# One place moved to each half of the split weights: four instead of three for high and low parts, eight instead of ten for raw chunks of the experts' weights

## The chip, the cores and the metric

The kernel runs on one core of a Trainium2 chip. The metric is the device time of one execution in microseconds (us). The engines are named as in the profile: PE (TensorE, matrix products), PEld (its loading of stationary operands), DVE (VectorE), ACT (ScalarE), POOL (GpSimd) and SP (SyncE, which here only issues loads). L1316 is line 1316 of the kernel.

## The reference, cut to what matters

The kernel computes one layer of a decoder trunk for 512 tokens of width 1024: a token mixer of three branches, cross-attention, and a mixture of experts. Only the last is touched. Each token goes to 4 of 32 experts; an expert is a gated unit with a 1024x2048 and a 1024x1024 weight matrix in float32.

```
def moe_ffn(h, w_router, b_router, w_gu, b_gu, w_down, b_down):
    ...
    top_logits, top_idx = lax.top_k(logits, TOP_K)
    gates = jax.nn.softmax(top_logits.astype(jnp.float32), axis=-1).astype(t.dtype)
    ...
    def expert_block(args):
        xb, e = args
        gu = xb @ w_gu[e] + b_gu[e]
        return clamped_swiglu(gu[:, :D_FF], gu[:, D_FF:]) @ w_down[e] + b_down[e]
    ...
    y = jnp.zeros_like(t).at[tok_of].add(y_assign)
```

## The kernel before

**Chunks.** The experts' weights (384 MB) come as 384 chunks of 128x2048 float32, 1 MB each (8 KB per partition): eight for w_gu and four for w_down of an expert. `chunk_raw` (L1312) takes the next raw place and issues the load on SP's queue (L1316). The raw places are taken in turn from three pools: mraw0 with 2, mraw1 with 5 and mraw2 with 3, ten in all. A load that takes a place waits on SP, in order, until the last reader of that place ten chunks earlier is done.

**High and low parts.** For most chunks `chunk` (L1319) makes two operands that PE can multiply at its faster rate: ACT writes the high part mhi (L114), DVE subtracts it from the raw chunk and writes the low part mlo (L115). Both have three places (pool mhl). PE multiplies the high part with the high and low part of the tokens, the low part with the high part alone. A place is free again when PE has read it.

```
def hl_tile(self, j):
    pool, k, n = self.hl_turns[self.nhl[j] % len(self.hl_turns)]
    self.nhl[j] += 1
    t = ("mhi", "mlo")[j] + str(k)
    return pool.tile([128, 2048], F32R, name=t, tag=t, bufs=n)
```

**Two streams.** Experts are walked in two interleaved streams (`run`, L1543). Stream A has 17 experts, 14 of them with 96 rows of tokens; their w_gu gate half is partly multiplied straight from the raw chunk in plain float32 (`mraw,xF` in the rows). Stream B has 15 experts with 64 rows; there the high and low part of the tokens stand side by side as 128 rows (xgN). From about 1443 us on the work repeats every two experts: 24 chunks, one wide expert and one narrow one. A repetition is called a period below.

**What an expert needs besides chunks.** `prepare` (L1409) finds the expert's tokens: DVE compares slot numbers (Pe, L1232 or L1237), PE multiplies (pt<-V,Pe), DVE writes the table of rows GI and the gates GT (L1244, L1245), and POOL issues an indirect load that gathers the tokens' rows, 4 KB each (L1592, xg<-x_scratch,GI). PE transposes what was gathered (L110, pt<-ident,xg: xg_10070, called xg1 in the program, for stream A, and xg0 for stream B), and ACT and DVE split it (xgT and xF, or xgN). After `gate` (L1444) and `up` (L1462) the product g is transposed (pt<-ident,g) and split into hT, in two halves. After `down` (L1494) the output o of an expert is added to memory by an indirect store with addition, also issued by POOL (L1597, y_scratch<-o,GI).

**What sets the order.** These steps are not written into the loop where they run: `when` (L1383) notes a step with the number of splits and of chunks after which it is due, and `flush` (L1388) runs what is due, placed behind the newest split. The program is then put in order for each engine by a scheduler that uses times of its own, and each engine runs its instructions in that order. POOL's indirect loads and stores thus stand in one row too.

Of the kernel before, what the change touches and what calls it, by code (L numbers as in the profile page):

```python
# [92 lines left out]
class K:  # L93
# [1236 lines left out]
    def moe(self, wk, xgp):  # L1330
# [212 lines left out]
        def run(T):  # L1543
# [3 lines left out]
            for e, f, g in zip(T, [*T[1:], None], [*T[2:], None, None]):  # L1547
# [10 lines left out]
                if f not in (None, 31):  # L1558
                    yield from up(f)

        A, B = [run(T) for T in STREAMS]
        a = b = True
        for n in range(999):
# [233 lines left out]
    def run(self):  # L1797
        nc, I, ctx = self.nc, self.I, self.ctx
        self.raws = []
        self.hls = []  # L1800

        self.newest = {}
        self.ths = {}
        dram = lambda n, shape, dt=F32: nc.dram_tensor(n, shape, dt, kind="Internal").ap()
        self.x0d = dram("x0_scratch", (NT, 128, D))
        self.kTd = dram("kx_scratch", (128, KT, 256))
        self.x2d = dram("x2_scratch", (S, D))
        self.y2d = dram("y2_scratch", (S, D))
        self.tabd = dram("blk_scratch", (NX, 2))
        self.tabid = dram("blki_scratch", (NX, 1), I32)  # L1810
        self.setup()
        wpc = ExitStack()
        self.wp = wpc.enter_context(self.pool("w", bufs=3, side="right"))
        with ExitStack() as pc:
            self.pd = pc.enter_context(self.pool("pd", bufs=2, space=PSUM))
            self.ps = pc.enter_context(self.pool("ps", bufs=2, space=PSUM))
            self.pt = pc.enter_context(self.pool("pt", bufs=2, space=PSUM))
            self.po = pc.enter_context(self.pool("po", bufs=2, space=PSUM))
            mgc, xc = ExitStack(), ExitStack()
            self.mixers(mgc)  # L1820
            xT = xc.enter_context(self.pool("xT"))
            x1p = xc.enter_context(self.pool("x1"))
            R, xh = self.mix_out(x1p, xT)
            mgc.close()
            rc = ExitStack()

            def before_xo():
                wpc.close()
                self.mp = ctx.enter_context(self.pool("moe", side="right"))
                self.moe_setup(self.mp)  # L1830
                self.hl_pool(ctx.enter_context(self.pool("mhl", side="right")), 3)
                self.raw_pool(ctx.enter_context(self.pool("mraw0", side="right")), 2)

            def x2_done(i):
                if i == 0:
                    self.route_setup(rc.enter_context(self.pool("route")))
                nc.scalar.dma_start(self.x2d[i * 128:i * 128 + 128], R[i])
                nc.gpsimd.dma_start(self.y2d[i * 128:i * 128 + 128], R[i])
                self.route_tile(i, R[i])
                if "x2" in self.dbg:  # L1840
                    nc.sync.dma_start(self.dbg["x2"][i], R[i])
            self.xattn(R, xh, xT, ExitStack(), x2_done, before_xo)
            self.route()
            rc.close()
            self.gp2.close()
            xc.close()
        with ExitStack() as pc:
            self.pd = pc.enter_context(self.pool("pd", bufs=3, space=PSUM))
            self.pt = pc.enter_context(self.pool("pt", bufs=2, space=PSUM))
            xgp = pc.enter_context(self.pool("mxg"))  # L1850
            self.raw_pool(pc.enter_context(self.pool("mraw2")), 3)
            wk = pc.enter_context(self.pool("mwk"))
            self.moe(wk, xgp)
        self.more_blocks()
# [74 lines left out]
```

## Time and profile before

| | |
|---|---|
| time, median of 3 runs | 2422.8 us (2421.11 to 2424.07) |
| the profiled execution | 2424.83 us, of which span 2423.0 us |
| mean granted clock of PE | 0.965 of full speed |
| busy share of the span: PE, DVE, ACT, POOL | 93%, 72%, 53%, 17% |
| the experts' stage | about 1240 to 2423 us |
| loads | 531 MB in all, 384 MB of them the chunks |

The busy shares are means over stages that differ. PE's matrix products are pipelined and their ends modelled, so a busy PE says little; what an engine waits for, and between which two instructions, says more.

### The profile page before, as it was taken

To read this page: it belongs to the slowest core of one execution; us is meant where nothing else is said; L and a number is where in the kernel's file an instruction comes from. 1 tells how busy PE (TensorE), PEld (TensorE's weight loads), DVE (VectorE), ACT (ScalarE), POOL (GpSimd) and SP (SyncE) were. 2 spreads that over 40 slices of the span, in tenths; PEclk is the share of its full clock that TensorE was granted. 3 is DMA by queue.
4 is the path that set the end of the run, shared out by engine and by line. 5 is a ranking of instruction groups with operands and counts; after the bars stand their busy time and mean duration, and the time that the engine had idled before them with its cause. 6 is when DMAs were issued, how large, how long until landed. Compare 5 with 4: busy or idle time off the path is not lost.

```text
span 2423.0 us, 29556 instructions
## 1 busy us (share of the span) xinstructions
PE 2245.9 (93%) x10449; PEld 1666.4 (69%) x10449; DVE 1745.0 (72%) x2696; ACT 1295.6 (53%) x1744; POOL 403.9 (17%) x289
## 2 busy tenths in 40 slices
PE   7999899999999998999899999999999999999893
PEld 6778789878887776787776666565666666555552
DVE  6465577546668675535757998888888888889886
ACT  3444433345557563123235777666667666667662
POOL 2000133121010002001301251202212211221102
PEclk9999899999999999999779999999999999999996
DMA  8432222332221214243639999999999999999992
GB/s 262 113 83 70 66 65 67 97 97 70 70 68 37 62 35 126 74 131 120 246 120 359 386 390 383 371 371 368 370 368 361 363 377 366 366 365 342 374 326 77
DMA packets 258792, 530.84 MB, mean 219 GB/s; under 512 B 31047, under 2 KB 143940, under 8 KB 258512
## 3 DMA queue, kind: packets, MB, share of 16 engines
q1 hardware_dynamic: 244720, 487.89, 57.3%
q0 software_dynamic: 11904, 33.61, 5.6%
q10 hardware_dynamic: 2016, 7.41, 0.9%
q8 instruction: 84, 1.38, 0.2%
q14 instruction: 68, 0.56, 0.1%
HBM read 507.70 MB, written 19.40 MB: 218 GB/s over the span
## 4 chain that ended last, share of the span: by engine, by line
PE 62%; DVE 15%; issue 12%; DMA 5%; ACT 4%; POOL 1%; DVEq 0%; SPq 0%; ACTq 0%; POOLq 0%
PE pd L107 49%; DVE mlo L115 7%; PE ps L107 5%; PE pt L110 4%; PE po L107 4%; ACT mhi L114 3%; DMA y_scratch<-o,GI 2%; PE pt L107 1%; DVE wlo L115 1%; DVE g L1476 1%; DMA mraw<-in_w_xo_dram 1%; DVE g L1453 1%; DMA raw<-in_w_xq_dram 1%; DMA xg<-x_scratch,GI 0%; DVE g L1459 0%
## 5 line engine op out<-in xcount | busy, mean ns | idle before, releaser
L115 DVE TENSOR_TENSOR mlo<-mraw,mhi 128x2048 fp32r<-128x2048 f32 x320 | 726.7, 2280 | 72.1 <-ACT mhi L114 67.2
L114 ACT ACTIVATE mhi<-mraw 128x2048 fp32r<-128x2048 f32 x323 | 606.6, 1908 | 66.9 <-PE pd L107 42.0
L107 PE MATMUL pd<-hT,whi 128*128 128x512 f32 (+1 forms) x1136 | 296.8, 406 | 9.0 <-DVE qs L352 4.2
L1597 POOL DMA_INDIRECT y_scratch<-o,GI x31 | 157.7, 5087 | 755.7 <-DVE o L1508 378.4
L107 PEld LDWEIGHTS pd<-hT,whi 128*128 128x128 f32 (+1 forms) x1136 | 213.2, 192 | 58.5 <-issue 3.9
L115 DVE TENSOR_TENSOR wlo<-raw,whi 128x1024 fp32r<-128x1024 f32 (+1 forms) x121 | 155.5, 1288 | 126.9 <-ACT whi L114 59.8
L107 PE MATMUL pd<-mraw,xF 128*96 128x512 f32 (+1 forms) x512 | 231.1, 593 | 0.0
L114 ACT ACTIVATE whi<-raw 128x1024 fp32r<-128x1024 f32 (+1 forms) x121 | 127.2, 1058 | 187.4 <-PE pd L107 144.4
L107 PE MATMUL pd<-mhi,hT 128*96 128x512 f32 (+1 forms) x720 | 193.0, 402 | 21.0 <-DVE hT L115 14.3
L107 PEld LDWEIGHTS pd<-mhi,hT 128*96 128x96 f32 (+1 forms) x720 | 121.4, 173 | 70.4 <-DVE hT L115 16.8
L107 PE MATMUL pd<-mlo,hT 128*128 128x512 f32 (+1 forms) x496 | 149.5, 423 | 18.0 <-DVE mlo L115 18.0
L107 PEld LDWEIGHTS pd<-mraw,xF 128*96 128x96 f32 (+1 forms) x512 | 79.5, 158 | 113.3 <-issue 107.4
L107 PE MATMUL pd<-hT,wlo 128*128 128x512 f32 (+1 forms) x568 | 156.6, 401 | 0.0
L107 PE MATMUL pd<-mlo,xgN 128*128 128x512 f32 x480 | 137.2, 407 | 12.3 <-DVE mlo L115 11.4
L107 PE MATMUL pd<-mhi,xgT 128*96 128x512 f32 (+1 forms) x544 | 141.2, 400 | 3.3 <-ACT mhi L114 1.6
L107 PE MATMUL pd<-mhi,xgN 128*128 128x512 f32 x480 | 134.6, 402 | 0.1
L107 PEld LDWEIGHTS pd<-mlo,hT 128*128 128x128 f32 (+1 forms) x496 | 83.6, 179 | 72.4 <-DVE mlo L115 40.8
L107 PEld LDWEIGHTS pd<-hT,wlo 128*128 128x128 f32 (+1 forms) x568 | 104.9, 188 | 22.8 <-issue 0.7
L107 PEld LDWEIGHTS pd<-mhi,xgT 128*96 128x96 f32 (+1 forms) x544 | 90.5, 168 | 40.5 <-ACT mhi L114 2.4
L107 PEld LDWEIGHTS pd<-mlo,xgN 128*128 128x128 f32 x480 | 86.0, 188 | 46.8 <-DVE mlo L115 26.3
L115 DVE TENSOR_TENSOR ptl<-pt,pth 128x512 fp32r<-128x512 f32 (+4 forms) x144 | 84.6, 606 | 44.0 <-ACT pth L114 42.9
L114 ACT ACTIVATE pth<-pt 128x512 fp32r<-128x512 f32 (+4 forms) x144 | 72.3, 527 | 69.2 <-PE pt L110 68.3
(445 smaller groups left out, 3812.7 us busy)
## 6 DMA issues: line engine op xcount, KB each, us to landing
mraw<-in_w_gu_dram SPq DMA_DIRECT2D x256, 1024.0 KB, 9.1
mraw<-in_w_down_dram SPq DMA_DIRECT2D x128, 1024.0 KB, 7.7
raw<-in_w_in_dram SPq DMA_DIRECT2D x78, 512.0 KB, 4.1
kd<-kd POOLq DMA_DIRECT2D x20, 256.0 KB, 4.2
raw<-in_w_xk_dram SPq DMA_DIRECT2D x8, 512.0 KB, 9.1
raw<-in_w_in_dram SPq DMA_DIRECT2D x16, 256.0 KB, 3.5
raw<-in_w_br_b_dram SPq DMA_DIRECT2D x8, 512.0 KB, 3.9
raw<-in_w_br_c_dram SPq DMA_DIRECT2D x8, 512.0 KB, 3.9
```

The costliest lines, as they stand in the source:

```text
L107: return self.nc.tensor.matmul(out, l, r, start=start, stop=stop)
L110: self.nc.tensor.transpose(out, in_, self.ident[:n, :n])
L114: return (self.nc.scalar.activation(hi, src, AF.Copy), (eng or self.nc.vector).tensor_tensor(lo, src, hi.bitcast(F32), op=ALU.subtract))
L115: (eng or self.nc.vector).tensor_tensor(lo, src, hi.bitcast(F32), op=ALU.subtract))
L1453: nc.vector.tensor_scalar(g, P, 7.0, None, op0=ALU.min)
L1476: nc.vector.tensor_tensor(g[:, c], u, g[:, c], op=ALU.mult)
L1597: self.nc.gpsimd.indirect_dma_start(out=self.y2d, out_offset=bass.IndirectOffsetOnAxis(ap=GI, axis=0), in_=o, in_offset=None, bounds_check ...
```

## The change

In the scope that runs the experts' stage, the third raw pool shrinks from three places to one, and a pool with one place for a high part and one for a low part is opened beside it. A raw place, a high place and a low place are of one size (8 KB per partition), so the memory is the same.

```diff
             xgp = pc.enter_context(self.pool("mxg"))
-            self.raw_pool(pc.enter_context(self.pool("mraw2")), 3)
+            self.raw_pool(pc.enter_context(self.pool("mraw2")), 1)
+            self.hl_pool(pc.enter_context(self.pool("mhl2")), 1)
             wk = pc.enter_context(self.pool("mwk"))
             self.moe(wk, xgp)
```

Since the scheduler orders the program anew, rows move on all engines. The numbers behind names are those of the program's tiles; those of one chunk are three higher in the changed program (mhi_13309 becomes mhi_13312). Three places follow, all in the same period.

On POOL, one row per indirect load or store, before (o_13217 is the output of a wide expert, o_13442 that of a narrow one):

```order
L1597 DMA y2_scratch<-o_12939,GI_10071 512x1024
L1592 DMA xg1_10070<-x2_scratch,GI_10071 96x1024
L1597 DMA y2_scratch<-o_13217,GI_10071 512x1024
L1592 DMA xg0_10793<-x2_scratch,GI_10071 64x1024
L1597 DMA y2_scratch<-o_13442,GI_10071 512x1024
L1592 DMA xg1_10070<-x2_scratch,GI_10071 96x1024
```

And now:

```order
L1592 DMA xg1_10070<-x2_scratch,GI_10071 96x1024
L1597 DMA y2_scratch<-o_12942,GI_10071 512x1024
L1592 DMA xg0_10796<-x2_scratch,GI_10071 64x1024
L1597 DMA y2_scratch<-o_13220,GI_10071 512x1024
L1592 DMA xg1_10070<-x2_scratch,GI_10071 96x1024
L1597 DMA y2_scratch<-o_13445,GI_10071 512x1024
```

Each gather has moved ahead of the store that stood before it: the gather of xg0 no longer stands behind the store of the wide expert's output.

On DVE, the second half of the period, before (hT_13177 is the narrow expert's hT):

```order
L115 TENSOR_TENSOR mlo_13226<-mraw_13223,mhi_13225 128x2048
L1244 TENSOR_SCALAR GI<-pt 128x1
L1245 TENSOR_REDUCE GT<-pt 128x1
L115 TENSOR_TENSOR mlo_13245<-mraw_13242,mhi_13244 128x2048
L115 TENSOR_TENSOR hT_13177<-pt,hT_13177 128x4x64 x2
L115 TENSOR_TENSOR mlo_13259<-mraw_13256,mhi_13258 128x2048
L119 ISA g_10795<-pd,u 64x512
L115 TENSOR_TENSOR mlo_13296<-mraw_13293,mhi_13295 128x2048
L119 ISA g_10795<-pd,u 64x512
L115 TENSOR_TENSOR mlo_13310<-mraw_13307,mhi_13309 128x2048
```

And now:

```order
L1244 TENSOR_SCALAR GI<-pt 128x1
L1245 TENSOR_REDUCE GT<-pt 128x1
L115 TENSOR_TENSOR hT_13180<-pt,hT_13180 128x4x64
L115 TENSOR_TENSOR mlo_13189<-mraw_13186,mhi_13188 128x2048
L115 TENSOR_TENSOR mlo_13207<-mraw_13204,mhi_13206 128x2048
L115 TENSOR_TENSOR hT_13180<-pt,hT_13180 128x4x64
L115 TENSOR_TENSOR mlo_13229<-mraw_13226,mhi_13228 128x2048
L115 TENSOR_TENSOR mlo_13248<-mraw_13245,mhi_13247 128x2048
L115 TENSOR_TENSOR mlo_13262<-mraw_13259,mhi_13261 128x2048
L119 ISA g_10798<-pd,u 64x512
L115 TENSOR_TENSOR mlo_13299<-mraw_13296,mhi_13298 128x2048
L119 ISA g_10798<-pd,u 64x512
```

The table GI, GT of the next narrow expert stands three low parts earlier, and the halves of hT stand apart, each ahead of a different low part.

On PE, around the transposes of the narrow expert's tokens (xg), before:

```order
L107 MATMUL pd<-mlo_13310,xgT 96x512 x4
L107 MATMUL pd<-Be,OHe 96x512 x2
L107 MATMUL pd<-mhi_13334,hT_13177 128x512 x4
L107 MATMUL pd<-mraw_13356,xF 96x512 x4
L107 MATMUL pd<-mlo_13335,hT_13177 128x512 x4
L107 MATMUL pd<-mhi_13366,hT_13177 128x512 x4
L107 MATMUL pd<-mraw_13380,xF 96x512 x4
L107 MATMUL pd<-mlo_13367,hT_13177 128x512 x4
L107 MATMUL pd<-Be,OHe 128x512 x2
L107 MATMUL pd<-mhi_13395,xgN 128x512 x4
L107 MATMUL pd<-mraw_13422,xF 96x512 x4
L110 MATMUL pt<-ident,xg_10793 128x64 x8
```

And now:

```order
L107 MATMUL pd<-mhi_13261,xgT 96x512 x8
L107 MATMUL pd<-mlo_13262,xgT 96x512 x4
L107 MATMUL pd<-mhi_13298,hT_13180 128x512 x4
L107 MATMUL pd<-mlo_13299,hT_13180 128x512 x4
L107 MATMUL pd<-mhi_13312,xgT 96x512 x8
L110 MATMUL pt<-ident,xg_10796 128x64 x8
L107 MATMUL pd<-mlo_13313,xgT 96x512 x4
L107 MATMUL pd<-Be,OHe 96x512 x2
```

These transposes have moved from behind the third raw chunk's products to before the low part of mraw_13307 (13310 now): twelve times in the program, once per period.

## Rows read from the trace of the kernel before

**Rows 1.** Windows: from:to, length, busy us of each engine, PEclk, DMA share, GB/s

```profile
1400.00:1450.00 50.00, 50.00 (x217) 35.05 (x217) 48.47 (x40) 39.59 (x32) 27.77 (x2) 1.00 1.02 401
1657.00:1728.00 71.00, 66.78 (x276) 43.01 (x275) 59.66 (x51) 47.13 (x41) 13.57 (x4) 1.00 1.01 366
```

**Rows 2.** Waits, 1350 to 2350: who <- for whom: us, times, longest

```profile
PE pd L107 <- DVE mlo L115: 39.1, 66, 2.0
...
PE pd L107 <- DVE hT L115: 13.7, 12, 2.5
...
PE pd L107 <- ACT mhi L114: 8.3, 23, 1.6
...
PE pt L110 <- DMA xg<-x_scratch,GI: 1.2, 1, 1.2
```

**Rows 3.** Page, loads: KB each, median us from issue to landing

```profile
mraw<-in_w_gu_dram SPq DMA_DIRECT2D x256, 1024.0 KB, 9.1
mraw<-in_w_down_dram SPq DMA_DIRECT2D x128, 1024.0 KB, 7.7
```

**Rows 4.** Timeline of DVE: start, us, line, work, [idle before <- releaser]

```profile
1683.02 2.29 DVE L115 TENSOR_TENSOR mlo<-mraw,mhi 128x2048 fp32r<-128x2048 f32 x1 [1.24 <-ACT mhi L114]
1685.23 0.55 DVE L115 TENSOR_TENSOR hT<-pt,hT 128x384 fp32r<-128x384 f32 x1
1685.69 2.28 DVE L115 TENSOR_TENSOR mlo<-mraw,mhi 128x2048 fp32r<-128x2048 f32 x1
...
1714.87 0.16 DVE L1244 TENSOR_SCALAR GI<-pt 128x1 int32<-128x1 f32 x1 [0.81 <-PE pt L107]
...
1715.01 2.28 DVE L115 TENSOR_TENSOR mlo<-mraw,mhi 128x2048 fp32r<-128x2048 f32 x1
1717.21 0.75 DVE L115 TENSOR_TENSOR hT<-pt,hT 128x256 fp32r<-128x256 f32 x2
1718.96 2.29 DVE L115 TENSOR_TENSOR mlo<-mraw,mhi 128x2048 fp32r<-128x2048 f32 x1 [1.00 <-ACT mhi L114]
1721.17 0.68 DVE L119 CUSTOM_DVE_ANT_0 g<-pd,u 64x512 f32<-64x512 f32 x1
```

**Rows 5.** Timeline of PE, the same period and the start of the next

```profile
1726.99 1.09 PE L107 MATMUL pd<-mlo,xgT 128*96 128x512 f32 x4
...
1743.89 0.71 PE L110 MATMUL pt<-ident,xg 64*128 64x64 f32 x8
...
1754.53 2.10 PE L107 MATMUL pd<-mhi,hT 128*96 128x512 f32 x8 [0.17 <-ACT mhi L114]
```

**Rows 6.** Timeline of ACT, around the wide expert's hT

```profile
1682.90 0.49 ACT L114 ACTIVATE hT<-pt 128x384 fp32r<-128x384 f32 x1
1683.29 3.72 ACT L114 ACTIVATE mhi<-mraw 128x2048 fp32r<-128x2048 f32 x2
```

**Rows 7.** Timeline of POOL: indirect stores (L1597) and gathers (L1592)

```profile
1368.35 4.87 POOL L1592 DMA_INDIRECT xg<-x_scratch,GI  x1 [0.30 <-issue]
...
1421.92 24.38 POOL L1597 DMA_INDIRECT y_scratch<-o,GI  x1 [25.89 <-ACT o L1505]
...
1706.69 8.69 POOL L1597 DMA_INDIRECT y_scratch<-o,GI  x1 [24.98 <-ACT o L1505]
1715.68 2.46 POOL L1592 DMA_INDIRECT xg<-x_scratch,GI  x1 [0.30 <-issue]
...
1752.20 0.99 POOL L1592 DMA_INDIRECT xg<-x_scratch,GI  x1 [3.97 <-DVE GT L1245]
```

**Rows 8.** Timeline of DVE, 1355 to 1375

```profile
1367.88 4.48 DVE L115 TENSOR_TENSOR mlo<-mraw,mhi 128x2048 fp32r<-128x2048 f32 x2
1372.28 0.68 DVE L119 CUSTOM_DVE_ANT_0 g<-pd,u 64x512 f32<-64x512 f32 x1
1372.88 2.28 DVE L115 TENSOR_TENSOR mlo<-mraw,mhi 128x2048 fp32r<-128x2048 f32 x1
```

**Rows 9.** Line L1592, 1715 to 1717: the gather of rows 7

```profile
DMA to landing us min/median/max: 10.1/10.1/10.1
```

## The prediction

> **What bounds the kernel now.** I read the windows first. Up to 1450 us of the experts' stage PE has no idle time (50.00 of 50.00 busy); from then on it is short of 4.2 us in every 71, at the full clock [rows 1]. The waits from 1350 to 2350 name whom PE waits for: mostly a low part from DVE, then the split of hT, then a high part from ACT, 61 us together [rows 2]. That is the most that any better supply of split weights could return. The DMA engines are counted busy throughout, which proves no limit: they moved 401 GB/s in one window and 366 in another at the same share [rows 1], since loads queue up as soon as a place is free.
>
> Then the timelines of DVE and PE over one period, 71.5 us: the low part at 1683.02 and the product that follows it recur at 1754.53 [rows 4, 5]. The reader is to see two halves. From 1683 on DVE works back to back, with PE in step with it, except for two gaps: 0.81 us, in which the table of the next narrow expert waits for PE, and 1.00 us before a low part whose high part ACT made late [rows 4]. From 1726.99 to 1754.53 PE does the raw chunks' slow products and is the one waited for [rows 5].
>
> **The change part by part.** *A fourth place for the halves.* By the order of the program the high and low parts stand nearly where they stood against PE's products, so the place buys little run-ahead. What the new order moves is the rest of a period, and there I price it. I count from the start of the low part at 1683.02, called zero.
>
> *DVE's stretch.* The first L119 of rows 4 (1721.17) starts at 38.15. What stands between is the same set of instructions before and after, except that the second half of the wide hT now comes ahead of zero: 1685.69 - 1685.23 = 0.46. The table's products stand earlier on PE, so the 0.81 gap goes, and the two halves of the narrow hT are spread out, so the 1.00 gap can go. Together 2.27: L119 starts at 35.9, and PE reaches the next product but one wide chunk on, at 1726.99 - 1683.02 = 43.97 before, at 41.7.
>
> *PE's stretch.* 1754.53 - 1726.99 = 27.5 us. The transposes of xg0 leave it and stand right ahead of it (0.71 us, no change in the sum). Zero comes when the high part behind hT is made, and hT's second half now stands ahead of that too: I add ACT's time for a half, 1683.29 - 1682.90 = 0.39 [rows 6].
>
> Net 2.27 - 0.39 = 1.9 us per period. This supposes a DVE without any gap; before it had 1.8 us of them. I let 0.4 come back and take **1.5 us**, with 0.5 and 1.9 as bounds. The new place of the transposes occurs twelve times: 12 x 1.5 = 18 us.
>
> *The gather of xg0.* This is what the gain rests on. Before, it was issued at 1715.68, landed 10.1 us later, at 1725.8 [rows 7, 9], and PE transposed at 1743.89 [rows 5]: 18 us to spare. Now PE wants it at 41.7. The gather waits for the table, which moves with it: it stood at 1714.87, 31.85 after zero; less three low parts at 1717.21 - 1715.01 = 2.20 each, the 0.46 and the 0.81, it is at 24.0, and the gather starts by about 24.3. A gather that POOL runs freely takes 0.99, the one at 1715.68 took 2.46 [rows 7], so landing is 10.1 - 2.46 = 7.6 after its end. A free one lands at 33; the latest end without a wait is 41.7 - 7.6 = 34.1.
>
> But POOL doesn't run freely beside DVE. A store took 8.69 us, another 24.38; the gather at 1368.35 took 4.87 and ended at 1373.22, 0.86 after the end of a run of low parts (1372.36), with a gap of 1372.88 - 1372.28 = 0.60 filled by L119 [rows 7, 8]; that at 1715.68 ended 0.85 after its low part, with 0.75 of hT [rows 7, 4]. So POOL's indirect DMAs get done when DVE stops subtracting, for 0.6 us at least. After 24.3 the new order offers: half an hT (0.75 / 2 = 0.4) before the first low part, another at about 28.8, then three low parts in a row, and L119 with 0.6 at 35.9. If either half hT is enough, or DVE has a gap of some tenths up to 34, nothing waits. I take it so, because two openings of 0.4 and the gap that I left in the sum lie before 34; it is close to even. Priced both ways: 0, or the first rival below.
>
> The Trainium skill, "SBUF — State Buffer", section "Who interferes with whom", speaks against the change: a DVE instruction that reads two SBUF operands contends with a GpSimd instruction that reads SBUF, and whichever issues first keeps the shared port until its end. Rows 7 and 8 agree for the case that DVE is first. By that rule a gather that starts ahead of the low part would stop DVE instead, for up to its 0.99; a period would then gain about 1.9 - 0.8 = 1.1 and the kernel 13 us. No row of before shows that case; it lies in the forecast's own range, and the case of DVE being first is the first rival, priced from rows.
>
> *Stores.* The wide expert's store now stands behind the gather. Nobody near waits for it; it has the whole PE stretch, where DVE pauses. 0.
>
> *Two raw places fewer.* A place is refilled every ten chunks now, 10 x 71.5 / 24 = 29.8 us, and every eight then, 23.8. A load takes 9.1 or 7.7 us to landing [rows 3], the split 1.9 and 2.28 [rows 6, 4], together 13.3; some 10 us are left for queueing and for the order in which places fall free. In the period this is thinnest at one chunk, whose high part is made 6 us before its low part, so a load late by a little is covered. I take 0; if the cover is gone, up to 2 us a period.
>
> *Bandwidth.* A period shortened to 70 us needs 366 x 71.5 / 70 = 374 GB/s, under the 401 of rows 1.
>
> *Start and end.* Loads move later by up to two chunks at the start, and one chunk is split earlier: 0 to 1 us, taken 0.5. The one wait of PE for a gather, 1.2 us [rows 2], goes with the old order. At the end two loads move behind four others: 0 to 3, taken 0. Up to 1450 PE is full, so nothing is gained there.
>
> **Sum.** -18 - 1.2 + 0.5 = -18.7, against the profiled 2424.8 (span 2423.0 and 1.8 around it): 2406.1. That execution lay 2.0 above the median of the runs shown, 2422.8, so I say **2404 us**. With 0.5 or 1.9 a period, and ends of 3: 2394 to 2418.
>
> **The rivals.** *First, slower: the gather gets through only at L119.* It then ends at 35.96 + 0.86 = 36.8 and lands at 44.4; PE, at 41.7, waits 2.7 with DVE waiting behind it for xgN, and nothing makes it up in PE's stretch. The period is 71.5 - 1.9 + 2.7 = 72.3, +0.8 or, with the 0.4, +1.2: 12 times that is 10 to 14 us, less 1.2: about 2433. For it: 0.4 is less than any opening that rows 7 and 8 show to be enough. It decides from an end of the gather later than 34.1, and turns the sign from 36.
>
> *Second, much slower: one opening of L119 isn't enough either.* The next is 2.8 us later (0.6 and 2.20): 34 us more, about 2466. If only the pause before xgN, near 45, lets it through, it lands near 54, PE waits 12 us a period: about 2540. For it: the 24.38 us of rows 7. Against it: that was a store; the gather of rows 8 passed at its first L119.
>
> *Third: the raw chunks bind.* Loads 2 us late per period with full effect, 24 us, eat the 18: about 2428. Against it: the 10 us above.
>
> *Fourth, nothing changes:* the gaps of DVE turn up at other instructions, for instance at a high part that ACT makes late behind a transpose. About 2422.
>
> **How the numbers follow.** Forecast 0.42; gather late at L119 0.25; later still 0.09; raw chunks 0.09; nothing 0.15. What can be told from no change is about 0.2%, 4.8 us. Faster: the forecast, 0.03 of the first rival (a quick landing) and 0.03 of the fourth: 0.48. Same: 0.07 of the first, 0.02 of the third and 0.1 of the fourth: 0.19. Slower: the rest, 0.33. The range takes in the forecast's own 2394 to 2418, the first, third and fourth rival and the first case of the second: 2394 to 2464; outside stays about 0.12.
>
> **What the profile after would show.** Right: a period of 69.6 to 71 us; the transposes of xg0 on PE without a wait; the gather of xg0 done within some 9 us of its table; no wait for a low part longer than the 0.7 of now; PE's waits for DVE down by a third or more. Wrong by the first two rivals: waits "PE pt <- DMA xg", twelve of 2 to 4 us or more, and gathers that take 12 us or longer. Wrong by the third: ACT's high parts waiting for mraw. Wrong by the fourth: the same 71.5 us with gaps of DVE under other names. What would upset the whole is a wait that none of these names, on ACT above all: it takes its instructions in order, and the transposes' splits now stand elsewhere in its row.

## The result, and the profile after

The changed kernel takes 2406.32 us (median of 5 runs, 2401.8 to 2411.22) against 2422.95 (2421.11 to 2424.42, 5 runs) for the kernel before: a ratio of 0.9932, 95% interval 0.9917 to 0.9947. The profiled execution took 2406.29 with a span of 2404.5 and the same granted clock, 0.965. So it is faster by 0.7%, 2.3 us from the forecast of 2404.

The windows of after, in the columns of [rows 1]; the second is about one period long:

```profile
1400.00:1450.00 50.00, 49.97 (x223) 34.95 (x222) 46.72 (x41) 36.26 (x32) 5.12 (x2) 1.00 1.03 392
1667.00:1737.00 70.00, 67.02 (x283) 43.83 (x282) 60.14 (x53) 47.58 (x40) 17.70 (x4) 1.00 1.01 372
```

PE is still full up to 1450, so nothing could be gained there. Later it lacks 2.98 us in 70 where it lacked 4.22 in 71. DMA moves 372 GB/s, where 374 was worked out.

The waits of after from 1350 to 2350, to be laid beside [rows 2]:

```profile
ACT mhi L114 <- DMA mraw<-in_w_gu_dram: 37.3, 11, 5.2
...
PE pd L107 <- DVE mlo L115: 32.5, 55, 2.0
...
PE pd L107 <- ACT mhi L114: 12.2, 26, 1.6
...
PE pt L110 <- DMA xg<-x_scratch,GI: 3.8, 1, 3.8
```

PE's wait for hT (13.7 before) is gone and the one for low parts fell from 39.1 to 32.5, while the one for high parts rose from 8.3 to 12.2. Two rows matter later: a single wait of 3.8 us for a gather, and ACT's waits for raw chunks, of which the view of before has none.

One period on DVE, counted as in [rows 4]; the columns are start, us, engine, line and work, and idle time before with its releaser. The last row is the next period's zero:

```profile
1676.03 4.49 DVE L115 TENSOR_TENSOR mlo<-mraw,mhi 128x2048 fp32r<-128x2048 f32 x2 [1.24 <-ACT mhi L114]
...
1699.92 0.14 DVE L1244 TENSOR_SCALAR GI<-pt 128x1 int32<-128x1 f32 x1
1699.99 0.14 DVE L1245 TENSOR_REDUCE GT<-pt 128x1 f32<-128x2 f32 x1
1700.06 0.41 DVE L115 TENSOR_TENSOR hT<-pt,hT 128x256 fp32r<-128x256 f32 x1
1700.39 4.48 DVE L115 TENSOR_TENSOR mlo<-mraw,mhi 128x2048 fp32r<-128x2048 f32 x2
1704.79 0.41 DVE L115 TENSOR_TENSOR hT<-pt,hT 128x256 fp32r<-128x256 f32 x1
1705.12 6.68 DVE L115 TENSOR_TENSOR mlo<-mraw,mhi 128x2048 fp32r<-128x2048 f32 x3
1711.73 0.68 DVE L119 CUSTOM_DVE_ANT_0 g<-pd,u 64x512 f32<-64x512 f32 x1
...
1745.66 4.49 DVE L115 TENSOR_TENSOR mlo<-mraw,mhi 128x2048 fp32r<-128x2048 f32 x2 [1.24 <-ACT mhi L114]
```

The period is 1745.66 - 1676.03 = 69.63 us (71.5 before). The rows from the table to L119 carry no idle time: the gaps of 0.81 and 1.00 have gone, and L119 starts at 1711.73 - 1676.03 = 35.70 (38.15 before).

PE in the same period, and once later:

```profile
1717.91 0.71 PE L110 MATMUL pt<-ident,xg 64*128 64x64 f32 x8
...
2139.43 1.09 PE L110 MATMUL pt<-ident,xg 64*128 64x64 f32 x8 [3.77 <-DMA xg<-x_scratch,GI]
```

The transposes of xg0 start at 41.88 after zero without a wait. From there to the next zero it is 69.63 - 41.88 = 27.75. From 24.0 after zero (1700.05) to the next zero PE waits for nothing. The kernel before had three waits for DVE in this part, 0.53 + 0.97 + 0.57 = 2.07 in all, and by as much PE is earlier behind them, 43.97 - 41.88 = 2.09:

```profile
1708.78 1.18 PE L107 MATMUL pd<-mlo,xgT 128*96 128x512 f32 x4 [0.53 <-DVE mlo L115]
...
1717.68 1.20 PE L107 MATMUL pd<-mhi,hT 128*128 128x512 f32 x4 [0.97 <-DVE hT L115]
...
1724.10 1.20 PE L107 MATMUL pd<-mlo,hT 128*128 128x512 f32 x4 [0.57 <-DVE mlo L115]
```

POOL, to be laid beside [rows 7], and then the landing of the gather at 1700.34 (the view of its line):

```profile
1700.34 5.38 POOL L1592 DMA_INDIRECT xg<-x_scratch,GI  x1 [29.07 <-DVE GT L1245]
...
2117.99 15.11 POOL L1592 DMA_INDIRECT xg<-x_scratch,GI  x1 [28.78 <-DVE GT L1245]
```

```profile
DMA to landing us min/median/max: 13.4/13.4/13.4
```

The gather ends 0.85 after the low part that ends at 1700.39 + 4.48 = 1704.87. Half an hT makes a pause of 1705.12 - 1704.87 = 0.25 there, so the gather ends when the next low part has already run for 0.6. It lands at 1713.8, 4.1 ahead of the transposes. That is the weak point of the forecast, and here it held. At 2117.99 it did not: the gather took 15.11 and PE waited 3.77.

**The account of the 18.5 us.** Seven periods from one gather of xg0 to another took 2073.12 - 1572.75 = 500.4 before and 2048.50 - 1561.02 = 487.5 after, 1.84 less each. By 2096 PE reaches the same work (its products with Be, which both kernels have) 17.5 us sooner. One period on, behind the late gather, it is 13: PE waited 3.77, and in the stretch after that its granted clock was 0.50 of full speed, the lower of its two levels, 1.2 GHz (columns of [rows 1]):

```profile
2139.40:2145.00 5.60, 5.57 (x19) 3.79 (x19) 3.08 (x4) 4.83 (x5) 0.98 (x1) 0.50 1.04 383
```

By 2360 it is 14 to 15, and at the end some 4 more come back: the last store but one took 3.20 in place of 6.51. From the first gather to the end it is 2423.0 - 1230.13 = 1192.9 before and 2404.5 - 1229.51 = 1175.0 after.

### The profile page after: what moved, and what is told of

Its sections match the earlier page's. It is cut to its first block, busy times and chain, and to the rows that moved or that the text cites. A ratio compares the mean times of both kernels' runs of the same rounds, so it can differ in the third digit from the quotient of the medians.

```text
span 2404.5 us, 29547 instructions
## 1 busy us (share of the span) xinstructions
PE 2247.1 (93%) x10449; PEld 1671.5 (70%) x10449; DVE 1742.7 (72%) x2696; ACT 1294.9 (54%) x1744; POOL 424.3 (18%) x289
## 5 line engine op out<-in xcount | busy, mean ns | idle before, releaser
L1592 POOL DMA_INDIRECT xg<-x_scratch,GI x31 | 94.3, 3042 | 694.6 <-DVE GT L1245 646.0
L1597 POOL DMA_INDIRECT y_scratch<-o,GI x31 | 143.5, 4630 | 196.3 <-DVE o L1508 141.6
L107 PEld LDWEIGHTS pd<-mlo,hT 128*128 128x128 f32 (+1 forms) x496 | 84.1, 177 | 62.7 <-DVE mlo L115 27.9
```

The lines of the kernel that those rows point to most:

```text
L107: return self.nc.tensor.matmul(out, l, r, start=start, stop=stop)
L1592: self.nc.gpsimd.indirect_dma_start(out=xg[:n], out_offset=None, in_=self.x2d, in_offset=bass.IndirectOffsetOnAxis(ap=self.GI[:n, e:e + 1] ...
L1597: self.nc.gpsimd.indirect_dma_start(out=self.y2d, out_offset=bass.IndirectOffsetOnAxis(ap=GI, axis=0), in_=o, in_offset=None, bounds_check ...
```

## The experiments

My theory was that of the prediction: the gain is DVE's two gaps and the half hT, and it is real as long as the gather of xg0 comes through in the 0.26 us that the second half of hT leaves between low parts. Rivals were that the fourth place for the halves does it, that the place of xg0's transposes does, that fewer raw places cost something that the gain covers, and chance in the order of the start. Below, "period" is the distance of two gathers of xg0, and every ratio is to the kernel before, run on the same chip. Two changed kernels that ran on different chips are compared by their ratios; 0.01 is 24 us.

**Is it the fourth place?** Eight raw places, three for the halves:

```diff
             self.raw_pool(pc.enter_context(self.pool("mraw2")), 1)
-            self.hl_pool(pc.enter_context(self.pool("mhl2")), 1)
```

> Eight raw places and three places each for high and low parts: the change without its fourth place. In the repeated part of the program the order on PE, DVE and ACT is the same, row for row, as in the changed kernel. Theory (the gain comes from the order of the period, which the smaller number of raw places brought about; the fourth place is not used): a period of 69.6 to 69.8 us, as in the changed kernel (69.65), and 2400 to 2411 us in all. Rival (the fourth place lets DVE and ACT run ahead and is what pays): a period of 71 us or more, with high or low parts that wait for PE to free a place, and 2420 us or more.

It took 2412.05 us, 1 us more than expected, ratio 0.996 (0.9944 to 0.9975), with a period of 1770.60 - 1700.90 = 69.70. The rows of the repeated period stand in the same order as with the fourth place, so that place does nothing there. Most of the time lost against the change lies elsewhere: PE waits 9.0 us for gathers, once at 1373 and once at 2142, where the change waits 3.8 in all.

**Is it the place of the transposes?** The change, with the transposes of xg0 due ten chunks on, as they nearly were before:

```diff
-                            when(0, transpose, 5)
+                            when(0, transpose, 5 if s == 0 else 10)
```

> The changed kernel with the transposes of the narrow expert's tokens noted as due ten chunks on instead of five: they go back into PE's stretch, four products later, and all the rest of the period keeps its order. Theory (the gain is DVE's two gaps and the half hT; the place of the transposes only decides how late the gather may be): the period stays at 69.6 to 69.9 us, no wait of PE for a gather even where one is late, 2400 to 2406 us. Rival (the transposes ahead of PE's stretch are what pays): the period goes back toward 71.5 us, 2420 us or more.

2405.34 us, 0.9923 (0.9904 to 0.9942), period 69.66. The gain doesn't come from where the transposes stand, and the gather at 2123 took 15.11 again without PE waiting for it. The 4 us saved there went to a wait of 4.4 near the start, at 1309, for the split of a narrow expert's tokens (xgN).

**Is it eight?** Nine raw places and three for the halves (the third raw pool has two places):

```diff
-            self.raw_pool(pc.enter_context(self.pool("mraw2")), 3)
+            self.raw_pool(pc.enter_context(self.pool("mraw2")), 2)
```

> Nine raw places, three for the split parts. The order is between the two kernels: the transposes of xg0 are in PE's stretch, behind its first raw chunk; the table stands where the changed kernel has it, but the first half of the narrow hT comes behind a low part. Theory (gaps of DVE): both gaps go, a period of 69.6 to 70.2 us, no wait for a gather, 2402 to 2412 us. Rival (eight raw places or the fourth split place or the early transposes are needed): nearer to 71.5 us, 2418 us or more.

2399.93 us, 2 us less than expected, 0.9905 (0.9884 to 0.9927), period 69.71. All gathers of xg0 in the repeated part took 5.37 or 5.38, and PE waits for a gather once, 3.16 us near the start, where no wait was expected. So one raw place fewer already gives the whole gain per period, with nothing put in its place; what remains between these versions is which gather comes late.

**Do fewer raw places bind?** The change with one raw place less again, seven, and four for the halves:

```diff
-            self.raw_pool(pc.enter_context(self.pool("mraw2")), 1)
             self.hl_pool(pc.enter_context(self.pool("mhl2")), 1)
```

> Seven raw places and four for the split parts: one raw place fewer than the changed kernel, with an order of the period close to its. Theory (raw places have room to spare, a place comes round every 7 x 69.65 / 24 = 20.3 us against 13.3 us of load and split): high parts wait for data on ACT longer than in the changed kernel, where eleven such waits made 37 us from 1350 to 2350, but PE hardly more: 2402 to 2414 us. Rival (eight places are the least that carries the loads): loads 1 to 3 us late in each period reach PE, 2418 to 2445 us.

2486.28 us, 1.0255 (1.0231 to 1.028): slower by 61 us, which neither case of the expectation had, period 1732.35 - 1653.42 = 78.93. One period of it on POOL, PE and DVE, and the wait of PE from 1350 to 2350:

```profile
1653.42 15.12 POOL L1592 DMA_INDIRECT xg<-x_scratch,GI  x1 [29.16 <-DVE GT L1245]
```

```profile
1675.37 1.08 PE L110 MATMUL pt<-ident,xg 64*128 64x64 f32 x8 [7.09 <-DMA xg<-x_scratch,GI]
```

```profile
1657.88 0.41 DVE L115 TENSOR_TENSOR hT<-pt,hT 128x256 fp32r<-128x256 f32 x1
1658.22 6.67 DVE L115 TENSOR_TENSOR mlo<-mraw,mhi 128x2048 fp32r<-128x2048 f32 x3
1664.82 0.67 DVE L119 CUSTOM_DVE_ANT_0 g<-pd,u 64x512 f32<-64x512 f32 x1
1665.42 2.27 DVE L115 TENSOR_TENSOR mlo<-mraw,mhi 128x2048 fp32r<-128x2048 f32 x1
1667.62 0.67 DVE L119 CUSTOM_DVE_ANT_0 g<-pd,u 64x512 f32<-64x512 f32 x1
```

```profile
PE pt L110 <- DMA xg<-x_scratch,GI: 68.7, 10, 7.5
```

This is the mechanism of the prediction's first and second rivals: neither the half hT nor the first L119 let the gather through. It ended 0.85 after the low part that ends at 1667.69, at the second L119. The transposes also stand two products, some 3 us, earlier than in the change. The waits come to 68.7 us, of a loss of 61 to the kernel before and some 78 to the change. Each wait has a second price. In the stretch in which PE comes back after standing for 7.09 us its granted clock was 0.50, the lower level again:

```profile
1673.42:1678.42 5.00, 3.05 (x13) 2.52 (x14) 1.42 (x3) 2.31 (x4) 0.00 (x0) 0.50 1.03 316
```

From 1653.42 to 1732.35 PE is busy 68.95 us. The next kernel does the same work without the wait, from 1699.64 to 1769.41, in 66.86: 2.1 us less. ACT's waits for raw chunks are 8.0 us in all.

**So is the late gather all of it?** The same seven places, with the transposes of xg0 ten chunks on, so that nothing waits for the gather:

```diff
-                            when(0, transpose, 5)
+                            when(0, transpose, 5 if s == 0 else 10)
```

> Seven raw places and four for the split parts as before, but the transposes of xg0 due ten chunks on instead of five, so that they stand in PE's stretch again. The run with seven raw places took 2486 us, with a period of 78.5 us and a wait of PE for the gather of xg0 of about 7 us in each of ten periods; its gathers took 15.1 us. Theory (the late gather is the whole cause, seven raw places carry the loads): the gathers stay as slow, PE no longer waits for them, the period is 69.6 to 70.2 us and the time 2400 to 2412 us. Rival (seven places bind and the gather's wait only shows it): a period above 72 us, 2430 us or more, with ACT's high parts waiting for data instead.

2400.46 us, 0.9905 (0.9885 to 0.9924), period 69.77, although the gathers still take 15.12. The wait, with the clock that it cost, was the whole of it, and seven raw places carry the loads, with 35.7 us of waits of ACT for them that PE doesn't feel.

**Can the pause be made longer?** Seven places as in the slow kernel, and the low part of the second half of the narrow hT is written twice, with the same values. That is one more DVE instruction a period; all other rows of the repeated part stand in the same order:

```diff
-                    self.split_T(Ps, H)
+                    self.split_T(Ps, H, again=s == 1 and e != 31)
...
             self.hilo(P, X[0][sl], X[1][sl])
+            if again and a == 1:
+                self.nc.vector.tensor_tensor(X[1][sl], P, X[0][sl].bitcast(F32), op=ALU.subtract)
```

> Seven raw places and four split places again (2486 us, a period of 78.5 us, gathers of xg0 of 15.1 us for which PE waits about 7 us), with one instruction more per narrow expert on DVE: the low part of the second half of its hT is written twice, so the pause of DVE between two low parts there is about 0.6 us instead of 0.26. PE's and ACT's order is the same. Theory (the gather is held while DVE subtracts from two SBUF operands, and a pause of 0.36 us or more lets it through): the gather takes 5.4 to 5.7 us, PE no longer waits for it, the period is 69.8 to 70.6 us and the time 2403 to 2418 us, although DVE has 0.33 us more to do per period. Rival (the gather is slow for another reason and its end beside a pause of DVE is chance): still 15 us, a period of 78.5 to 79 us, 2486 us or more.

2398.99 us, 0.9901 (0.9883 to 0.9918): some 86 us less than without the extra instruction, and 4 under the range expected. DVE and POOL of one period:

```profile
1632.98 4.48 DVE L115 TENSOR_TENSOR mlo<-mraw,mhi 128x2048 fp32r<-128x2048 f32 x2
1637.38 0.41 DVE L115 TENSOR_TENSOR hT<-pt,hT 128x256 fp32r<-128x256 f32 x1
1637.82 0.42 DVE L1616 TENSOR_TENSOR hT<-pt,hT 128x256 fp32r<-128x256 f32 x1
1638.16 6.68 DVE L115 TENSOR_TENSOR mlo<-mraw,mhi 128x2048 fp32r<-128x2048 f32 x3
```

```profile
1632.92 5.38 POOL L1592 DMA_INDIRECT xg<-x_scratch,GI  x1 [29.18 <-DVE GT L1245]
```

The first low parts end at 1632.98 + 4.48 = 1637.46. The pause is now 1638.16 - 1637.46 = 0.70, the gather takes 5.37 or 5.38 in every period, and no transpose waits.

**Or does any extra instruction do it?** The same instruction for the first half (`a == 0`), which gives two pauses of 0.26 instead of one long one:

> The same extra instruction, but for the first half of hT, and it stands between the first two low parts after the gather starts: two pauses of about 0.26 us instead of one of 0.6, the same work on DVE. If what the gather has done in one pause counts for the next, as with nine raw places, where it met two pauses of 0.26 us and took 5.4 us: 5.4 us, no wait of PE, 2403 to 2418 us. If one pause has to be long enough for the whole: 15 us as without it, and 2480 us or more.

2492.38 us, 1.0287 (1.0268 to 1.0307), a period of 79.0 in the mean. POOL, PE's wait from 1350 to 2350, and DVE:

```profile
1647.60 15.45 POOL L1592 DMA_INDIRECT xg<-x_scratch,GI  x1 [29.16 <-DVE GT L1245]
```

```profile
PE pt L110 <- DMA xg<-x_scratch,GI: 71.3, 10, 7.9
```

```profile
1647.66 2.27 DVE L115 TENSOR_TENSOR mlo<-mraw,mhi 128x2048 fp32r<-128x2048 f32 x1
1649.85 0.41 DVE L1616 TENSOR_TENSOR hT<-pt,hT 128x256 fp32r<-128x256 f32 x1
1650.19 2.27 DVE L115 TENSOR_TENSOR mlo<-mraw,mhi 128x2048 fp32r<-128x2048 f32 x1
1652.39 0.41 DVE L115 TENSOR_TENSOR hT<-pt,hT 128x256 fp32r<-128x256 f32 x1
1652.72 6.68 DVE L115 TENSOR_TENSOR mlo<-mraw,mhi 128x2048 fp32r<-128x2048 f32 x3
```

The same extra work, and nothing gained: at this place in the row one longer pause let the gather through, and two short ones did not.

**The long pause in the change itself,** with the edit for the second half:

> The changed kernel with the extra instruction of the pause of 0.6 us (second half of hT written twice). Theory: the one gather of 15.1 us near 2118 us takes 5.4 us or so, PE's wait of 4 us there goes; DVE has 0.33 us more per period, so periods of 69.7 to 70.0 us: the stage from its first product to the end takes 1160 to 1163 us instead of 1162.5, about the same time in all, 2403 to 2407 us. Rival (DVE sets the period alone): 0.33 us more in each of twelve periods, 4 us, 2408 us or more.

2400.1 us, 0.9903 (0.9883 to 0.9922), period 69.80. That is 3 us under the forecast range. The gather near 2118 takes 5.37, and PE waits for no gather any more. The instruction costs 0.17 a period (69.80 against 69.63) and saves the late gather. The first L119 starts 0.45 later than in the change (36.15 after zero against 35.70), so not all of what DVE wins or loses in this stretch reaches the period: PE, which waits for nothing there, had some room. This version, like those of nine places and of seven with the long pause or late transposes, has a lower median than both kernels. The intervals of these four overlap, and their upper ends lie inside the change's own, 0.9917 to 0.9947, so they are ahead of it by about 0.3% at the median and not proven to be.

**Ten raw places in a like order?** The kernel before, with the transposes of xg0 due after four chunks:

```diff
-                            when(0, transpose, 5)
+                            when(0, transpose, 5 if s == 0 else 4)
```

> The kernel before with its ten raw and three split places, and the transposes of xg0 due four chunks on instead of five. The scheduler puts the next narrow expert's table two low parts earlier than before, xg0's transposes one raw chunk earlier; the two halves of the narrow hT stay together. Theory (the gain is an order of the period in which DVE has no gap, not a number of places): the gap before the table goes, the one behind hT may stay: a period of 69.7 to 70.7 us, 2400 to 2414 us. Rival (ten raw places or three split places hold the period at 71.5 us): 2418 us or more.

The expectation missed: 2436.92 us, 1.0056 (1.0038 to 1.0074), period 71.90. DVE and ACT:

```profile
1709.94 0.16 DVE L1244 TENSOR_SCALAR GI<-pt 128x1 int32<-128x1 f32 x1 [0.34 <-PE pt L107]
...
1714.03 6.70 DVE L115 TENSOR_TENSOR mlo<-mraw,mhi 128x2048 fp32r<-128x2048 f32 x3 [1.00 <-ACT mhi L114]
```

```profile
1738.10 0.66 ACT L114 ACTIVATE xgN<-pt 128x256 fp32r<-128x256 f32 x2 [9.27 <-PE pt L110]
```

The table and the halves of hT moved two low parts earlier along with the transposes, but the halves stayed together. The gap before the table shrank from 0.81 to 0.34, the one behind the halves stayed at 1.00 (L119 at 37.21 after zero, which is 35.9 + 1.34). What DVE's stretch won, 38.15 - 37.21 = 0.94, was lost behind it: ACT stood 9.27 us before the split of xgN, the next in its row, and its high part behind that came 0.72 late for PE. Some 9 us more went at the start, with a wait of 6.2 for a gather and a store of 25.5. So this run doesn't tell what the gaps alone are worth. What bears on it is a comparison of all kernels: in every repeated period of the kernels with 69.6 to 69.8 us DVE has no idle time between zero and that L119, and in the kernel before it has 1.8 us. No run put one gap back by itself. An order of ten places with the rows of the change was not built, so whether ten places forbid that order, or the scheduler only didn't choose it, is open.

**Is the time of the change chance?** The same kernel once more:

> The changed kernel once more, as it is. Its runs spread from 2401.8 to 2411.2 us. Theory (the repeated part is the same to 0.1 us in every execution, the one late gather at about 2118 us comes at its place in the program, and the spread is made ahead of the experts' stage): again a period of 69.6 to 69.7 us, again one gather of 15.1 us at the same place, PE waiting about 4 us for it, and the stage's start at another time by some us. Rival (which gathers are late is chance): none late, or two and more, and the time moves with their number, 4 us each.

2406.33 us, 0.9923 (0.9905 to 0.994), with the one late gather at the same place (15.11 at 2122.49). Its profile has a span of 2409.4 against 2404.5, but from the first gather to the end the two take 1175.6 and 1175.0: the difference lies ahead of the experts' stage.

**A single late gather.** Nine places, with the transposes of xg0 two chunks later (due 7):

> Nine raw places, three for the split parts, and the transposes of xg0 due seven chunks on instead of five. The repeated part is the same, row for row, as with nine places and five chunks (2399.9 us, a period of 69.7 us), only the first 200 us of the stage are put in another order, where that run had a wait of 3.2 us for a gather. Theory: that wait goes, the rest stays: 2395 to 2401 us. Rival (the wait was hidden by what else is late there, or another takes its place): 2400 to 2405 us.

2412.84 us, 0.995 (0.9933 to 0.9968); this missed too. The period stayed at 69.70, but a gather near the start came late:

```profile
1370.83 14.88 POOL L1592 DMA_INDIRECT xg<-x_scratch,GI  x1 [0.30 <-issue]
```

```profile
1391.06 1.09 PE L110 MATMUL pt<-ident,xg 64*128 64x64 f32 x8 [12.00 <-DMA xg<-x_scratch,GI]
```

One late gather costs PE 12 us where it is needed soon. In the kernel with nine places and the old due number the wait was 3.16, and the difference is most of the 11 us by which this kernel lies above that one.

## Why the prediction was right

- **DVE's stretch, 2.27.** L119 at 35.70 (35.9 forecast), the transposes at 41.88 (41.7). Right, and as far as the rows tell for the reason given: both gaps gone, the half hT ahead of zero. That a gain in this stretch reaches the period needs that nothing behind it takes it back; the kernel with ten places and moved transposes won 0.94 here and had a period of 71.90.
- **PE's stretch, 27.9.** 27.75 measured. Right.
- **The net per period, 1.5 after 0.4 was let back.** This term was mis-sized: it is 1.84, near the upper bound of 1.9. No gap came back in DVE's stretch. It was multiplied by twelve; nine to ten periods gave it in full (17.5 us by 2096), so the product, 18, came out right by luck, with two errors that cancel.
- **The gather of xg0, close to even.** It started at 24.31 after zero (24.3), passed at the half hT's pause and landed 8.0 after its end (7.6). "Close to even" was no modesty: the same rows with 0.26 us fail once in the change and in every period with seven places, where the second rival's case, beyond the first L119, cost 61 us. The step that was shaky is "another half hT of 0.4 is an opening": 0.41 is the length of the instruction, between the low parts only 0.26 is left, and that is not reliably enough. The first rival as it was priced, an end at the first L119, came in none of the 34 late gathers of the repeated part in all runs; all ended at the second.
- **The wait for a gather, -1.2, start +0.5, end 0.** The early wait went; a late one of 3.8 came, and clock was lost behind it, which the sum lacked. At the end about 4 us came back, which it lacked too. From the first of the four loads of y to the end it is now 2404.5 - 2366.65 = 37.85, before 2423.0 - 2387.17 = 35.8: 2.0 more, inside the 0 to 3 allowed for the two loads that moved behind them. That these two cost it was not tried.
- **Two raw places fewer, 0.** The cover that was named did the work. Loads are late now, once in most periods, before the chunk whose high part stands ahead of its low part; ACT and PE of after show it:

```profile
1727.90 1.91 ACT L114 ACTIVATE mhi<-mraw 128x2048 fp32r<-128x2048 f32 x1 [5.24 <-DMA mraw<-in_w_gu_dram]
```

```profile
1720.95 3.59 PE L107 MATMUL pd<-mraw,xF 128*96 128x512 f32 x8
...
1726.25 3.60 PE L107 MATMUL pd<-mraw,xF 128*96 128x512 f32 x8
```

  ACT waits 5.24, PE is at the raw chunks' products meanwhile and waits for nothing. The third rival thus exists without a price, and with seven places still.
- **The rule of the Trainium skill, "SBUF — State Buffer", section "Who interferes with whom".** That whoever starts first holds the shared port fits where DVE was first. The gather at 1700.34 started 0.05 ahead of a low part, and by the rule, read as the prediction read it, it should have held DVE up for up to its 0.99; the two low parts took 4.48, as they do elsewhere [rows 8], and the gather was the one that waited. Here the measurement decides: DVE didn't lose the 0.8 us a period. At which moment the gather asks for the port no row shows, so an order of 0.05 us on two engines is not a sharp test.
- **What would show it.** Period 69.63 (69.6 to 71), PE's waits for DVE down from 52.8 to 34.4, of which 1.9 are for a table near the end, 35% (a third or more), no gather wait but one. One line failed: in the repeated period a low part was waited for up to 0.95 us (at 1692.91), where no wait longer than the 0.7 of before was expected. The longest from 1350 to 2350, 2.0 us near the end, is as before.

## What to carry to other kernels

Here a transfer that GpSimd issues beside a busy VectorE was priced by the pauses of VectorE between its instructions with two SBUF operands. So look for the pause that it must hit, don't count on the next one, and let nothing depend on a pause of a quarter of a microsecond: one instruction more, which cost the change 0.17 us a period, made a pause of 0.70 and took some 86 us off the kernel with seven places. When a pool's size changes, look first at what the new order does to gaps on the engine that sets the pace; the places themselves may do nothing, as the fourth one here. And move whoever consumes such a transfer away from it, if the order allows: with transposes five chunks later the same late gather cost nothing, neither the wait nor the clock behind it.

## What the runs showed of the hardware that was not expected

Of the gathers that took longer than 2 us, in all runs, all but one ended 0.82 to 0.89 us after the end of some low part; of which one was not settled. The same DVE rows, equal to 0.01 us, gave 5.38 us at 1700.34 and 15.11 at 2117.99 in the kernel after. In both the pause comes 4.53 us after the gather's start and lasts 0.25 to 0.26. What differs in the records is ACT, first at 1700 and then at 2118:

```profile
1697.01 3.71 ACT L114 ACTIVATE mhi<-mraw 128x2048 fp32r<-128x2048 f32 x2
1701.65 0.39 ACT L114 ACTIVATE hT<-pt 128x256 fp32r<-128x256 f32 x1 [0.94 <-PE pt L110]
...
2118.54 1.24 ACT L1505 ACTIVATE o<-pd,GT 96x512 f32<-96x512 f32 x2
```

ACT is idle soon after the gather starts in the first case and at work in the second, as it is in the repeated period with seven places. But with nine places the gather starts with ACT at work and still takes 5.38, in the second of two pauses of 0.26, and with seven places at 1425.44 it took 5.37 with ACT at work and a pause of 0.36. So ACT alone is not shown to be the cause, and it was not tried by itself.

The length of the pause is not the whole rule either. In the kernel of the last experiment, nine places and transposes due 7, the gather of 1370.83 that took 14.88 met these rows of DVE:

```profile
1370.37 4.48 DVE L115 TENSOR_TENSOR mlo<-mraw,mhi 128x2048 fp32r<-128x2048 f32 x2
...
1375.37 2.27 DVE L115 TENSOR_TENSOR mlo<-mraw,mhi 128x2048 fp32r<-128x2048 f32 x1
...
1381.38 1.27 DVE L1472 TENSOR_SCALAR u<-pd 96x512 f32<-96x512 f32 x2
1382.58 2.27 DVE L115 TENSOR_TENSOR mlo<-mraw,mhi 128x2048 fp32r<-128x2048 f32 x1
```

Its first pause, 1375.37 - (1370.37 + 4.48) = 0.52, comes 4.0 after its start and is filled by L119, as in [rows 8], where the gather took 4.87; here it did not let the gather through. Nor did the 1.1 us before 1382.58, in which DVE has no instruction with two SBUF operands. In all runs no gather took between 6.03 and 14.88 us, and the 35 late ones took 14.88 to 15.46, whatever pauses lay between: with seven places the first L119, with 0.53 us between low parts (1665.42 - 1664.89), let none through and the second did. A gather that missed its first pause thus lost some 10 us and not just the time to the next one; why is open. Pauses of 0.70, and the one of 0.36 with seven places, sufficed at the gather's first opening; those of 0.26 and 0.52 did so in some rows and not in others.
